# Gated linear attention: half of the diff projections between the scan's levels, one output norm for all chunks, half copies of k on ScalarE

## The chip, the cores and the metric

The kernel runs on one core of a Trainium2 chip. The metric is the device time of one execution in microseconds. Three runs of the kernel before took 2683.73, 2684.15 and 2686.27 us, so its time is the median, 2684.15 us.

## The reference

The reference computes two layers of a hybrid trunk on 640 tokens (128 context tokens and 512 latent tokens) of width 1024, in float32. A layer has a mixer and an MLP. The mixer projects the normed input once and splits the columns among three branches. Branch A is gated linear attention (GLA) over both directions, branch B is latent attention, branch C is differential attention. The three outputs are merged by sigmoid gates that are computed from the same input. What the change touches is the end of branch A and the start of branch C:

```python
def gla_branch(q, k, v, r, a_lr, w_a2, b_a, g_out, s0):
    ...
    o_f, s_f = gla_chunk_scan(q, k, v, g[:, :, 0], s0[:, 0])
    o_b, s_b = gla_chunk_scan(flip(q), flip(k), flip(v), flip(g[:, :, 1]), s0[:, 1])
    o = rms_norm(o_f + flip(o_b), g_out.astype(f32))
    y = o.reshape(B, S, W_A).astype(r.dtype) * jax.nn.silu(r)
...
(aq, ak, av, ar, aa, qd, kvd, kr, dq, dk, dv, gates) = jnp.split(h @ lp['w_in'], offsets, axis=-1)
q_c = rms_norm(dq.reshape(B, S, H_C, 2, D_C), lp['g_diff_q'])
k_c = rms_norm(dk.reshape(B, S, H_C, 2, D_C), lp['g_diff_k'])
...
g_a, g_b, g_c = jnp.split(jax.nn.sigmoid(gates), N_BRANCH, axis=-1)
merged = g_a * (y_a @ lp['w_o_gla']) + g_b * (y_b @ lp['w_o_mla']) + g_c * (y_c @ lp['w_o_diff'])
```

Inside a chunk the scan's decayed attention is exact: for each pair of positions the decay between them is a difference of running sums of g.

## The kernel before

Every float32 matmul against weights is done as three matmuls on a high and a low half of each operand (`mm3`, L101 to L103). The halves of a weight are made after its load: the high one by a cast on ACT (L94), the low one by a subtraction on DVE (L96). All DMAs of the parts shown here are issued by SP, in one queue.

The order of the work is the order in which the Python code emits it, refined by a scheduler that works by priorities when the program is built; at run time each engine takes its own list in order. Between the steps of a branch the code emits filling work for TensorE with `fill(n)`. It takes n pieces from a list of generators: first the four blocks of the gate r of branch A (`gla_r`), then blocks of the merge's gates (`gates_early`). A piece is 24 matmuls that fill one PSUM tile, of 384 columns for the first half of the tokens and 256 for the second, then a tanh on ACT and a store. What has not been emitted when the merge comes is computed there. A layer emits 49 pieces ahead of the merge, three after each chunk of the scan.

The scan of branch A goes through five chunks of 128 positions (`gla_chunk`), each of them through seven levels of halving block sizes. In a level POOL makes differences of the running sums (L509, L510), ACT takes their exponential (L511), DVE multiplies q (L518) and k (L524) by it, PE multiplies the two for four heads (L527) and DVE copies the result into the chunk's matrix under a mask (L531). At the last level, of block size one, half of k is only copied, on DVE (L522), and half of q is doubled on ACT (L520). At the chunk's end PE multiplies the matrix by v (L541) and q by the state (L543). Then the output norm follows: a square on ACT (L545), a sum on DVE (L547), an inverse root in twelve small operations on DVE (`rsqrt`, L123 to L130), the scaling (L551), four transposes on PE (L554), a load of the gate r into "ya" (L556), the product with it (L557), and the store (L558).

After the scan the diff attention starts with its first half of heads: the projections of k, of q and of v (`diff_proj`, fifteen steps of 24 matmuls of 256 columns, each with an eviction by ACT, L385), the norm and rotation of k and q (`diff_prep`), three filling pieces, and then scores and attention (L953).

Of the kernel before, what the change touches and what calls it, by code (L numbers as in the profile page):

```python
# [11 lines left out]
F32 = mybir.dt.float32  # L12
# [22 lines left out]
MLA_FILL = (1, 0, 1, 0, 0, 0, 1, 1, 1, 1, 1, 1, 1, 1, 1, 1)  # L35
DIFF_FILL = (0, 2)
# [16 lines left out]
    "gla_q": ("gla", 1), "gla_k": ("gla", 1), "gla_es": ("gla", 1), "gla_p": ("gla", 10), "gla_v": ("gla", 5),  # L53
    "wa2": ("gla", 1), "aT": ("gla", 2), "gla_t0": ("gla", 2), "gla_t1": ("gla", 2),
# [6 lines left out]
    "tabdq": ("dif", 1), "tabdk": ("dif", 1), "df_q": ("dif", 5), "df_k": ("dfr", 5), "df_v": ("dif", 10),  # L61
# [10 lines left out]
class Net:  # L72
# [316 lines left out]
    def gla_gates(self, l):  # L389
        nc = self.nc  # L390
        wa = self.S([33, 512], F32, "wa2")
# [3 lines left out]
        for tt in range(5):  # L395
            pt = self.P([128, 512], "gt")
            nc.tensor.transpose(pt[0:33, 0:128], self.aan[:, tt], self.ident)
            at = self.S([33, 128], F32, "aT")
# [26 lines left out]
    def gla_r(self, l, h, js):  # L425
        nc = self.nc
        for j in js:
            w = self.load_w(self.a["wfm"][l, 4 + j], [128, 8, 128])
            ws = [(w[0][:, k], w[1][:, k]) for k in range(8)]
            for c0, c1 in HALVES:  # L430
                p = self.P([128, 512], "f")
                n = c1 - c0
                self.gemm(p[:, :n], ws, h, c0, c1)
# [60 lines left out]
    def gla_chunk(self, l, c):  # L494
# [9 lines left out]
        for li, h in enumerate(LEVELS + (1,)):  # L504
# [45 lines left out]
        on = self.S([128, 4, 128], F32, "gla_o")  # L550
        nc.vector.tensor_tensor(on, o, r.unsqueeze(2).to_broadcast([128, 4, 128]), op=ALU.mult)  # L551
        p = self.P([128, 4, 128], "gt")
        for hd in range(4):
            nc.tensor.transpose(p[:, hd], on[:, hd], self.ident)  # L554
        y = self.S([128, 4, 128], F32, "ya")
        nc.sync.dma_start(y, self.yr[:, :, cs])  # L556
# [1049 lines left out]
```

## Time and profile before

| | |
|---|---|
| median of three runs | 2684.15 us |
| the profiled execution | 2684.53 us, its span 2682.7 us |
| PE busy | 2540.2 us (95%) |
| PEld busy (weight loads, beside PE) | 2429.5 us (91%) |
| DVE busy | 1712.2 us (64%) |
| ACT busy | 1142.2 us (43%) |
| POOL busy | 531.8 us (20%) |

The span is the time from the first to the last instruction on the chip; the 1.83 us beyond it lie around the program. An engine that is busy for 95% of the span can still be waiting for others for much of one stage, and another that is busy for 64% can be the one that is waited for there. So the shares are to be read by stage.

### The profile page before, as it was taken

The page shows a single profiled execution, that of the slowest core. Times are in us where ns is not written, and L with a number is a line of the kernel's source. Part 1 is how long each engine was busy: PE and PEld are TensorE (multiplying, and loading weights), DVE is VectorE, ACT ScalarE, POOL GpSimd, SP SyncE. Part 2 cuts the span into 40 slices and gives each one's busy share as a digit, 9 for nine tenths or more (in the row PEclk, how much of TensorE's full clock was granted, in tenths as well). Part 3 has the DMA queues.
Part 4 walks back from the last instruction along what each step waited for, and adds up shares of the span by engine and source line. Part 5 has one row for each costly group of instructions (what it writes and reads, how often), then busy time and mean ns, then how long its engine had stood idle before and what let it go on. Part 6 is the DMA issues. An engine that isn't in the chain of part 4 may idle for free.

```text
span 2682.7 us, 45820 instructions
## 1 busy us (share of the span) xinstructions
PE 2540.2 (95%) x17680; PEld 2429.5 (91%) x17680; DVE 1712.2 (64%) x3952; ACT 1142.2 (43%) x2287; POOL 531.8 (20%) x704
## 2 busy tenths in 40 slices
PE   6999997899998999999989999978999999999999
PEld 3988897789898999999989888878898999999999
DVE  6477649767688776766665775597685556333332
ACT  4476553356523342231335774533564334132231
POOL 3022115521032021020221211355100401010110
PEclk8999999999999999999999999999999999999999
DMA  6111212221275544444421112122113542222221
GB/s 247 44 51 63 66 62 73 72 76 56 84 257 199 162 138 153 149 150 150 150 77 54 44 57 80 49 80 78 60 57 129 192 143 78 79 72 79 71 79 48
DMA packets 112273, 268.87 MB, mean 100 GB/s; under 512 B 12534, under 2 KB 48374, under 8 KB 111288
## 3 DMA queue, kind: packets, MB, share of 16 engines
q1 hardware_dynamic: 112056, 265.95, 30.5%
q8 instruction: 139, 2.28, 0.4%
q14 instruction: 78, 0.64, 0.1%
HBM read 234.55 MB, written 31.36 MB: 99 GB/s over the span
## 4 chain that ended last, share of the span: by engine, by line
PE 70%; DVE 18%; ACT 5%; issue 3%; DMA 3%; POOL 1%; SPq 0%; DVEq 0%; ACTq 0%; POOLq 0%
PE g L103 17%; PE g L101 17%; PE g L102 17%; PE f L101 3%; PE f L103 2%; PE f L102 2%; DVE gla_z L518 2%; DVE wlo L96 2%; DVE mjunk L208 2%; PE y L991 1%; DVE gla_A L531 1%; PE g L787 1%; DMA modw<-wmod 1%; DVE gla_t L524 1%; PE g L983 1%
## 5 line engine op out<-in xcount | busy, mean ns | idle before, releaser
L96 DVE TENSOR_TENSOR wlo<-wraw,whi 128x1024 fp32r<-128x1024 f32 (+3 forms) x230 | 261.2, 1137 | 225.7 <-ACT whi L94 223.7
L94 ACT CAST whi<-wraw 128x1024 fp32r<-128x1024 f32 (+2 forms) x236 | 219.9, 932 | 398.5 <-PE g L102 306.5
L103 PE MATMUL g<-hh,wlo 128*128 128x384 f32 (+1 forms) x1056 | 331.2, 314 | 2.6 <-DVE wlo L96 2.6
L101 PE MATMUL g<-hh,whi 128*128 128x384 f32 (+1 forms) x1056 | 329.8, 312 | 1.9 <-ACT gth L1152 1.4
L102 PE MATMUL g<-hl,whi 128*128 128x384 f32 (+1 forms) x1056 | 329.7, 312 | 0.0
L1265 POOL TENSOR_TENSOR relu<-relu 128x256 f32<-128x256 f32 (+1 forms) x128 | 112.8, 882 | 801.4 <-ACT uh L1264 794.5
L208 DVE CUSTOM_DVE_ANT_0 mjunk<-modw,condb 128x1024 bf16<-128x1024 f32 x160 | 199.0, 1244 | 53.6 <-DMA modw<-wmod 52.9
L94 ACT CAST xhi<-xraw 128x1024 fp32r<-128x1024 f32 (+1 forms) x80 | 83.7, 1046 | 285.3 <-PE g L102 256.4
L103 PEld LDWEIGHTS g<-hh,wlo 128*128 128x128 f32 x1056 | 200.7, 190 | 3.3 <-DVE wlo L96 3.3
L101 PEld LDWEIGHTS g<-hh,whi 128*128 128x128 f32 x1056 | 201.0, 190 | 2.8 <-ACT gth L1152 1.8
L1214 DVE SCALAR_TENSOR_TENSOR x<-g,moda,x 128x256 f32<-128x256 f32 (+1 forms) x192 | 78.2, 435 | 193.3 <-PE g L103 193.3
L102 PEld LDWEIGHTS g<-hl,whi 128*128 128x128 f32 x1056 | 200.9, 190 | 0.1
L103 PE MATMUL g<-hh,xlo 128*128 128x384 f32 (+1 forms) x544 | 167.5, 308 | 0.0
L101 PE MATMUL g<-hh,xhi 128*128 128x384 f32 (+1 forms) x544 | 167.3, 307 | 0.0
L102 PE MATMUL g<-hl,xhi 128*128 128x384 f32 (+1 forms) x544 | 167.3, 307 | 0.0
L103 PE MATMUL g<-uh,wlo 128*128 128x384 f32 (+1 forms) x512 | 158.2, 309 | 0.0
L101 PE MATMUL g<-uh,whi 128*128 128x384 f32 (+1 forms) x512 | 158.2, 309 | 0.0
L102 PE MATMUL g<-ul,whi 128*128 128x384 f32 (+1 forms) x512 | 158.1, 309 | 0.0
L103 PE MATMUL g<-uh,xlo 128*128 128x384 f32 (+1 forms) x512 | 157.8, 308 | 0.0
L102 PE MATMUL g<-ul,xhi 128*128 128x384 f32 (+1 forms) x512 | 157.5, 308 | 0.0
L101 PE MATMUL g<-uh,xhi 128*128 128x384 f32 (+1 forms) x512 | 157.5, 308 | 0.0
L1201 POOL TENSOR_TENSOR x<-x,th 128x256 f32<-128x256 f32 x64 | 76.6, 1205 | 373.9 <-DVE th L1199 209.8
(449 smaller groups left out, 7859.3 us busy)
## 6 DMA issues: line engine op xcount, KB each, us to landing
modw<-wmod SPq DMA_DIRECT2D x80, 512.0 KB, 3.5
wraw<-w SPq DMA_DIRECT2D x64, 512.0 KB, 3.5
xraw<-w SPq DMA_DIRECT2D x64, 512.0 KB, 3.6
wraw<-wfm SPq DMA_DIRECT2D x62, 512.0 KB, 3.6
wraw<-wn SPq DMA_DIRECT2D x36, 512.0 KB, 3.6
wraw<-wo SPq DMA_DIRECT2D x48, 256.0 KB, 3.2
th<-gd SPq DMA_DIRECT2D x26, 320.0 KB, 3.1
gd<-gth SPq DMA_DIRECT2D x42, 192.0 KB, 1.9
```

What stands on the lines that cost most here:

```text
L94: nc.scalar.copy(hi, raw)
L96: eng.tensor_tensor(lo, raw, hi.bitcast(F32), op=ALU.subtract)
L101: mm(out, wh, xh, start=first, stop=False)
L102: mm(out, wh, xl, start=False, stop=False)
L103: mm(out, wl, xh, start=False, stop=last)
L208: nc.vector.tensor_tensor_reduce(out=junk, in0=w, in1=self.condb[:, s], scale=1.0, scalar=0.0, op0=ALU.mult, op1=ALU.add, accum_out=self.m ...
L518: nc.vector.tensor_tensor(q5[rs, :, :, u], qi[rs, :, :, u], d5[rs, :, :, u], op=ALU.mult)
L524: nc.vector.tensor_tensor(kt, k, dt, op=ALU.mult)
L531: nc.vector.copy_predicated(A, self.mask[:, li - 1].unsqueeze(1).to_broadcast([128, 4, 128]), p)
L1201: nc.gpsimd.tensor_tensor(mg[m][:, c0:c1], mg[m][:, c0:c1], t[:, c0:c1], op=ALU.add)
L1214: self.nc.vector.scalar_tensor_tensor(dst[:, p0:p1], p[:, p0 - c0:p1 - c0], self.moda[l][:, kind * 8 + m, s:s + 1], src[:, p0 - o:p1 - o], ...
L1265: nc.gpsimd.tensor_tensor(r[:, :n], r[:, :n], r[:, :n], op=ALU.mult)
```

## The change

The norm of the output leaves the chunk. A chunk now ends with a copy of its output into the place of its v, the square, and a sum that goes into one column of a common tile. After all chunks `gla_out` takes one inverse root for all and then scales, transposes, loads, multiplies and stores chunk by chunk. The three projections of the first half of the diff attention are emitted in steps after the levels 1, 3 and 5 of each chunk. Filling pieces can be left half done: a half is 12 matmuls, and every count of `fill` is now one of halves. Halves follow the levels 0, 2 and 4 and the chunk's end, so a chunk takes two whole pieces. The half copies of k are done by ACT. Some tiles change pools: the raw q and v of the first diff half to a pool that is open during the scan, and two tiles of the gates take the names of the scan's own.

```diff
 MLA_FILL = ...
-DIFF_FILL = (0, 2)
+DIFF_FILL = (0, 4)
+GLA_FILL = (0, 2, 4)
+GLA_PROJ = (1, 3, 5)
...
+    def gemm_part(self, out, ws, hs, c0, c1):
+        n = len(hs)
+        for k in range(n):
+            (wh, wl), (xh, xl) = ws[k], hs[k]
+            self.mm3(out, wh, wl, xh[:, c0:c1], xl[:, c0:c1], k == 0, k == n - 1)
+            if k == n // 2 - 1:
+                self.open_piece = True
+                yield
+                self.open_piece = False
+    def settle(self):
+        while self.open_piece:
+            self.fill(1)
...
-                    nc.vector.tensor_copy(k5[rs, :, :, 1 - u], ki[rs, :, :, 1 - u])
+                    nc.scalar.copy(k5[rs, :, :, 1 - u], ki[rs, :, :, 1 - u])
...
+            if li in GLA_PROJ:
+                while self.projq and next(self.projq[0], self) is self:
+                    self.projq.pop(0)
+            if li in GLA_FILL:
+                self.fill(1)
...
+        ov = self.v[c].rearrange("p (a b) -> p a b", a=4)
+        nc.scalar.copy(ov, o)
         sq = self.S([128, 4, 128], F32, "gla_o")
         nc.scalar.activation(sq, o, AF.Square)
-        ss = self.S([128, 4], F32, "gla_ss")
-        nc.vector.tensor_reduce(out=ss, in_=sq, axis=AX.X, op=ALU.add)
-        r = self.S([128, 4], F32, "gla_r")
-        self.rsqrt(r, ss, 1.0 / 128, 4)
-        ...
+        nc.vector.tensor_reduce(out=self.gss[:, c], in_=sq, axis=AX.X, op=ALU.add)
+
+    def gla_out(self):
+        r = self.S([128, 5, 4], F32, "gla_r")
+        self.rsqrt(..., self.gss..., 1.0 / 128, 20)
+        for c in range(5):
+            cs = slice(c * 128, c * 128 + 128)
+            ov = self.v[c].rearrange("p (a b) -> p a b", a=4)
+            on = self.S([128, 4, 128], F32, "gla_o")
+            nc.vector.tensor_tensor(on, ov, r[:, c].unsqueeze(2).to_broadcast([128, 4, 128]), op=ALU.mult)
+            p = self.P([128, 4, 128], "gt")
+            for hd in range(4):
+                nc.tensor.transpose(p[:, hd], on[:, hd], self.ident)
+            y = self.S([128, 4, 128], F32, "ya")
+            nc.sync.dma_start(y, self.yr[:, :, cs])
+            nc.vector.scalar_tensor_tensor(y, p, self.ghalf, y, op0=ALU.mult, op1=ALU.mult)
+            nc.sync.dma_start(self.yd[0][:, :, cs], y)
...
         for c in range(5):
             self.gla_chunk(l, c)
-            self.fill(3)
+            self.fill(1)
...
+        self.projq = [self.diff_proj(l, 0, i, h) for i in (1, 0, 2)]
         self.gla_chunks(l)
-        self.drain(self.diff_proj(l, 0, 1, h))
+        for g in self.projq:
+            self.drain(g)
+        self.gla_out()
+        self.settle()
...
-        self.drain(self.diff_proj(l, 0, 0, h))
         self.diff_prep(l, 0, 1)
         self.diff_prep(l, 0, 0)
-        self.drain(self.diff_proj(l, 0, 2, h))
-        self.fill(3)
+        self.fill(8)
         self.diff_attend(l, h)
```

How this stands in the lists of the engines is shown at three places. The line numbers of the changed kernel are higher (L96 is L99 there, L518 is L537, L524 is L543, L531 is L550, L547 is L572). The first place is DVE in the second half of the third chunk of the first layer. Before, the previous chunk's scaling and product with r (L551, L557) stand between the levels:

```order
L130 SCALAR_TENSOR_TENSOR gla_r<-rq_t_4976,gla_r 128x4
L518 TENSOR_TENSOR gla_z_4844<-gla_q,gla_t_5152 64x64x4
L551 TENSOR_TENSOR gla_o<-go,gla_r 128x512
L531 COPY_PREDICATED gla_A<-mask,go 128x512
L524 TENSOR_TENSOR gla_t_5156<-gla_k,gla_t_5152 128x512
L557 SCALAR_TENSOR_TENSOR ya<-gt,ghalf,ya 128x512
L518 TENSOR_TENSOR gla_z_4847<-gla_q,gla_t_5166 64x128x2 x2
L531 COPY_PREDICATED gla_A<-mask,go 128x512
L524 TENSOR_TENSOR gla_t_5170<-gla_k,gla_t_5166 128x512
L518 TENSOR_TENSOR gla_t_5185<-gla_q,gla_t_5180 64x256
L522 COPY gla_t_5184<-gla_k 64x256
L518 TENSOR_TENSOR gla_t_5185<-gla_q,gla_t_5180 64x256
```

After, only the sum of the previous chunk (L572) is left of it:

```order
L572 TENSOR_REDUCE gla_ss<-gla_o 128x4
L537 TENSOR_TENSOR gla_z_4856<-gla_q,gla_t_5519 64x32x8 x2
L543 TENSOR_TENSOR gla_t_5494<-gla_k,gla_t_5490 128x512
L99 TENSOR_TENSOR wlo<-wraw,whi 128x1024
L550 COPY_PREDICATED gla_A<-mask,go 128x512
L543 TENSOR_TENSOR gla_t_5523<-gla_k,gla_t_5519 128x512
L537 TENSOR_TENSOR gla_z_4859<-gla_q,gla_t_5559 64x64x4 x2
L537 TENSOR_TENSOR gla_z_4862<-gla_q,gla_t_5586 64x128x2 x2
L550 COPY_PREDICATED gla_A<-mask,go 128x512
L543 TENSOR_TENSOR gla_t_5563<-gla_k,gla_t_5559 128x512
L550 COPY_PREDICATED gla_A<-mask,go 128x512
```

The inverse root, the scaling, the product and the copies L522 are gone from the list here.

The second place is DVE behind the last chunk. Before, the end of the rsqrt of one chunk, its scaling and product, and then the sums for the norm of k (L896) and its low halves (L935):

```order
L129 SCALAR_TENSOR_TENSOR rq_t_5935<-rq_t_5935,rq_v_5933 128x4
L130 SCALAR_TENSOR_TENSOR gla_r<-rq_t_5935,gla_r 128x4
L551 TENSOR_TENSOR gla_o<-go,gla_r 128x512
L557 SCALAR_TENSOR_TENSOR ya<-gt,ghalf,ya 128x512
L1360 TENSOR_SCALAR ghalf<-vec 128x1
L896 TENSOR_REDUCE df_ss<-df_sq 128x4 x2
L935 TENSOR_TENSOR df_kl<-df_kc,df_k_6764 64x128
L935 TENSOR_TENSOR df_kl<-df_kc,df_k_6765 64x128
```

After, the end of the rsqrt for all chunks, then five scalings (L583) and five products with r (L589), and then the same sums (L929):

```order
L148 SCALAR_TENSOR_TENSOR rq_t_6211<-rq_t_6211,rq_v_6209 128x20
L149 SCALAR_TENSOR_TENSOR gla_r<-rq_t_6211,gla_r 128x20
L583 TENSOR_TENSOR gla_o<-gla_v,gla_r 128x512 x2
L589 SCALAR_TENSOR_TENSOR ya<-gt,ghalf,ya 128x512
L583 TENSOR_TENSOR gla_o<-gla_v,gla_r 128x512
L589 SCALAR_TENSOR_TENSOR ya<-gt,ghalf,ya 128x512
L583 TENSOR_TENSOR gla_o<-gla_v,gla_r 128x512 x2
L589 SCALAR_TENSOR_TENSOR ya<-gt,ghalf,ya 128x512 x3
L1395 TENSOR_SCALAR ghalf<-vec 128x1
L929 TENSOR_REDUCE df_ss<-df_sq 128x4 x3
```

All five chunks' products have moved ahead of the preparation of k and q.

The third place is SP's list at the end of the scan. Before, the stores of "ya" (L558) for the last three chunks and the load of "ya" (L556) for the last one, with stores of gates (L1153) and loads of weights (L91) between them; the other loads stand further up:

```order
L558 DMA yd_77<-ya 512x1x128
L556 DMA ya<-yr 128x4x128
L91 DMA wraw<-wn 128x1024
L1153 DMA gd_74<-gth 128x256
L1153 DMA gd_74<-gth 128x384
L91 DMA wraw<-wn 128x1024
L1153 DMA gd_74<-gth 128x256
L558 DMA yd_77<-ya 512x1x128
L1153 DMA gd_74<-gth 128x384
L91 DMA wraw<-wn 128x1024
L1153 DMA gd_74<-gth 128x256
L558 DMA yd_77<-ya 512x1x128
```

After, all five stores (L590) and the last three loads (L588) stand together, in turns; the loads of the first two chunks stand earlier:

```order
L94 DMA wraw<-wn 128x1024 x2
L1188 DMA gd_74<-gth 128x384
L94 DMA wraw<-wn 128x1024
L590 DMA yd_77<-ya 512x1x128 x2
L588 DMA ya<-yr 128x4x128 x2
L590 DMA yd_77<-ya 512x1x128 x2
L588 DMA ya<-yr 128x4x128
L590 DMA yd_77<-ya 512x1x128
```

The loads of chunks 2 to 4 have moved behind the stores of chunks 0 to 3. On PE the twenty transposes L586 stand in one group, ahead of the last four filling pieces.

## Rows read from the trace of the kernel before

**Rows 1.** The page, busy time of each engine

```profile
PE 2540.2 (95%) x17680; PEld 2429.5 (91%) x17680; DVE 1712.2 (64%) x3952; ACT 1142.2 (43%) x2287; POOL 531.8 (20%) x704
```

**Rows 2.** Busy time by stage, columns as its head names them

```profile
core 0: us, PE busy (x) PEld busy (x) DVE busy (x) ACT busy (x) POOL busy (x), PEclk, DMA share, GB/s
392.60:520.10 127.50, 101.14 (x713) 92.69 (x712) 117.37 (x223) 45.73 (x81) 69.55 (x98) 0.99 0.21 66
520.10:581.90 61.80, 60.08 (x469) 58.53 (x468) 35.37 (x98) 23.99 (x52) 15.29 (x28) 1.00 0.30 96
1722.80:1850.20 127.40, 102.73 (x713) 94.12 (x712) 117.18 (x223) 45.71 (x81) 69.49 (x98) 0.97 0.20 66
```

**Rows 3.** The waits in the scan: total, times, longest, us

```profile
ACT gla_t L511 <- POOL gla_t L510: 56.7, 24, 3.6
POOL gla_t L509 <- DVE gla_t L524: 23.3, 9, 3.6
```

**Rows 4.** Lines of DVE in the scan: busy us, mean ns, idle before

```profile
L522 DVE COPY gla_t<-gla_k 64x256 f32<-64x256 f32 x10 | 6.4, 637 | 0.0
L130 DVE SCALAR_TENSOR_TENSOR gla_r<-rq_t,gla_r 128x4 f32<-128x4 f32 x12 | 4.7, 394 | 0.0
...
L557 DVE SCALAR_TENSOR_TENSOR ya<-gt,ghalf,ya 128x512 f32<-128x512 f32 x4 | 3.0, 748 | 0.0
L547 DVE TENSOR_REDUCE gla_ss<-gla_o 128x4 f32<-128x512 f32 x4 | 2.7, 683 | 0.1
L551 DVE TENSOR_TENSOR gla_o<-go,gla_r 128x512 f32<-128x512 f32 x4 | 2.7, 683 | 0.1
...
L123 DVE TENSOR_SCALAR rq_v<-gla_ss 128x4 f32<-128x4 f32 x4 | 0.6, 160 | 0.0
```

**Rows 5.** Timeline of PE and PEld: start, length, instruction

```profile
394.46 0.28 PE L101 MATMUL g<-hh,whi 128*128 128x256 f32 x1
...
395.17 0.28 PE L101 MATMUL g<-hh,whi 128*128 128x256 f32 x1
...
401.20 0.34 PE L103 MATMUL g<-hh,wlo 128*128 128x384 f32 x1
...
402.59 0.34 PE L102 MATMUL g<-hl,whi 128*128 128x384 f32 x1
...
433.15 0.97 PEld L527 LDWEIGHTS go<-gla_z,gla_t 128*128 128x128 f32 x8
```

**Rows 6.** Lines of ACT in the scan

```profile
L520 ACT ACTIVATE gla_t<-gla_q 64x256 f32<-64x256 f32 x8 | 3.4, 424 | 0.0
L529 ACT COPY gla_A<-go 128x512 f32<-128x512 f32 x5 | 2.9, 578 | 0.0
```

**Rows 7.** Timeline of DVE, the last chunk's rsqrt

```profile
521.69 0.17 DVE L123 TENSOR_SCALAR rq_v<-gla_ss 128x4 f32<-128x4 f32 x1
...
523.87 0.16 DVE L130 SCALAR_TENSOR_TENSOR gla_r<-rq_t,gla_r 128x4 f32<-128x4 f32 x1
```

**Rows 8.** DMA issues: count, KB each, median us to landing

```profile
x<-gd SPq DMA_DIRECT2D x16, 320.0 KB, 5.7
...
ya<-yr SPq DMA_DIRECT2D x10, 256.0 KB, 3.3
yd<-ya SPq DMA_DIRECT2D x10, 256.0 KB, 2.6
```

**Rows 9.** Lines of DVE in the tail

```profile
L96 DVE TENSOR_TENSOR wlo<-wraw,whi 128x1024 fp32r<-128x1024 f32 x8 | 10.2, 1277 | 15.6 <-ACT whi L94 15.6
```

**Rows 10.** Busy time around a wait of PE, columns as in rows 2

```profile
472.20:474.50 2.30, 0.00 (x0) 0.00 (x1) 2.24 (x6) 1.46 (x4) 0.14 (x1) 0.94 0.46 178
474.50:477.50 3.00, 2.97 (x12) 2.97 (x13) 2.94 (x7) 0.63 (x1) 1.76 (x3) 0.50 0.01 4
```

**Rows 11.** Busy time in the merge of each layer

```profile
770.00:870.00 100.00, 87.78 (x578) 85.53 (x577) 82.34 (x132) 26.98 (x47) 41.51 (x32) 0.98 0.62 203
2070.00:2170.00 100.00, 99.78 (x688) 99.79 (x689) 57.81 (x97) 33.00 (x56) 32.65 (x31) 1.00 0.54 177
```

More of the change, by code (lines that the diff above doesn't have):

```diff
@@ L390, in gla_gates @@
         nc = self.nc
-        wa = self.S([33, 512], F32, "wa2")
+        wa = self.S([33, 512], F32, "gla_t2")
         nc.sync.dma_start(wa, self.a["wa2"][l])
@@ L432, in gla_r @@
                 n = c1 - c0
-                self.gemm(p[:, :n], ws, h, c0, c1)
+                yield from self.gemm_part(p[:, :n], ws, h, c0, c1)
                 t = self.S([128, 384], F32, "gth")
@@ L543, in gla_chunk @@
                 nc.tensor.matmul(o[:, hd], ei[:, hd], self.st[c][:, hd], start=False, stop=True)
+        ov = self.v[c].rearrange("p (a b) -> p a b", a=4)
+        nc.scalar.copy(ov, o)
         sq = self.S([128, 4, 128], F32, "gla_o")
         nc.scalar.activation(sq, o, AF.Square)
-        ss = self.S([128, 4], F32, "gla_ss")
-        nc.vector.tensor_reduce(out=ss, in_=sq, axis=AX.X, op=ALU.add)
-        r = self.S([128, 4], F32, "gla_r")
-        self.rsqrt(r, ss, 1.0 / 128, 4)
[L550 to L556, printed above, removed]
-        nc.vector.scalar_tensor_tensor(y, p, self.ghalf, y, op0=ALU.mult, op1=ALU.mult)
-        nc.sync.dma_start(self.yd[0][:, :, cs], y)
+        nc.vector.tensor_reduce(out=self.gss[:, c], in_=sq, axis=AX.X, op=ALU.add)
+    def gla_out(self):
+        nc = self.nc
+        r = self.S([128, 5, 4], F32, "gla_r")
+        self.rsqrt(r.rearrange("p a b -> p (a b)"), self.gss.rearrange("p a b -> p (a b)"), 1.0 / 128, 20)
+        for c in range(5):
[10 more added lines that the diff above has]
+            nc.sync.dma_start(self.yd[0][:, :, cs], y)
     def gla_chunks(self, l):
@@ L568, in gla_chunks @@
             self.qz[h] = z
+        self.gss = self.S([128, 5, 4], F32, "gla_ss")
         for c in range(5):
             self.gla_chunk(l, c)
-            self.fill(3)
+            self.fill(1)
     def mla_down(self, l, h):
@@ L880, in diff_proj @@
     def diff_proj(self, l, ch, i, h):
-        r = [self.S([128, 256], F32, f"df_{'qkv'[i]}") for t in range(5)]
+        r = [self.S([128, 256], F32, ("df_q", "df_k", f"df_v{ch}")[i]) for t in range(5)]
         self.raw[ch, i] = r
@@ L1084, in diff_attend @@
                 later.append(lambda ch=ch, yc=yc: store(ch, yc))
+        self.settle()
         self.ftag = "fg"
-        self.fill(1)
+        self.fill(2)
         for f in later:
@@ L1149, in gates_early @@
                 p = self.P([128, 512], self.ftag[c0 > 0])
-                self.gemm(p[:, :n], ws, h, c0, c1)
+                self.mid = True
+                yield from self.gemm_part(p[:, :n], ws, h, c0, c1)
                 t = self.S([128, 384], F32, "gth")
@@ L1366, in layer @@
         self.ftag = "ff"
-        self.mid, self.fillq, self.early, self.up, self.raw, self.rqd = False, [], set(), {}, {}, {}
+        self.mid, self.open_piece, self.fillq, self.early, self.up, self.raw, self.rqd = False, False, [], set(), {}, {}, {}
         fl, lat, latT, mla = ExitStack(), ExitStack(), ExitStack(), ExitStack()
@@ L1378, in layer @@
         self.pool_lo = False
-        self.fill(4)
+        self.fill(8)
         self.mla_latent(l)
@@ L1383, in layer @@
         mla.enter_context(self.pool("yb", "att", "mla"))
-        self.fill(1)
+        self.fill(2)
         self.drain(self.mla_keys(l, 0))
-        self.fill(1)
+        self.fill(2)
         self.mla_values(l, 0)
-        self.fill(1)
+        self.fill(2)
+        self.settle()
         ps.close()
@@ L1391, in layer @@
         self.mla_attend(l)
+        self.settle()
         for st in (mla, latT, ps):
@@ L1405, in layer @@
         self.gla_state(l)
-        self.fill(3)
+        self.fill(6)
+        self.projq = [self.diff_proj(l, 0, i, h) for i in (1, 0, 2)]
         self.gla_chunks(l)
-        self.drain(self.diff_proj(l, 0, 1, h))
+        for g in self.projq:
+            self.drain(g)
+        self.gla_out()
+        self.settle()
         for st in (gla, ps):
@@ L1414, in layer @@
         self.rope_tables((("dq", 0, 64, 0), ("dk", 64, 64, 0)))
-        self.drain(self.diff_proj(l, 0, 0, h))
+        nc.sync.dma_start(self.a["o_dv"][l, :, 0:256], self.raw[0, 2][4])
         self.diff_prep(l, 0, 1)
         self.diff_prep(l, 0, 0)
-        self.drain(self.diff_proj(l, 0, 2, h))
-        nc.sync.dma_start(self.a["o_dv"][l, :, 0:256], self.raw[0, 2][4])
-        self.fill(3)
+        self.fill(8)
         self.diff_attend(l, h)
-        while self.mid:
+        while self.mid or self.open_piece:
             self.fill(1)
```

10 lines of the change are left out of this document (5 added, 5 removed).

## The prediction

> **What bounds the kernel now.** I read the page first: TensorE (PE) is busy for 2540.2 of 2682.7 us [rows 1], so only stretches where it waits can give anything. The table by stage comes next [rows 2]. It has four stretches: in each layer from the end of the last state product (L480) to the last product of the scan (L541, "the scan"), and from there to the first score of the diff attention (L953, "the tail"). In the scan PE is busy for 101 of 127.5 us while VectorE (DVE) is busy for 117.4; in the tail PE is busy for 60.1 of 61.8. So the scan is bound by DVE and the tail by PE, and the second layer repeats it. The waits of the scan confirm the loop: ScalarE (ACT) waits 56.7 us for the differences that GpSimd (POOL) makes, and POOL 23.3 us for DVE's k product, whose buffer it refills [rows 3]. The lines of DVE show what loads it [rows 4].
>
> How much PE work is in there, without its waits? From start to start a matmul of 256 columns takes (395.17 - 394.46)/6 = 0.118 us, one of 384 columns (402.59 - 401.20)/8 = 0.174, a level's group of four 0.97 [rows 5]; for a product or a transpose of the same shape I take a quarter of that, 0.24, as an estimate. The order of before puts 172 filling matmuls of 384 columns, 170 of 256, 35 groups, 36 products and 16 transposes in the scan: 29.9 + 20.1 + 34.0 + 8.6 + 3.8 = 96 us, so 31 us of it are stalls. In the tail, where PE hardly waits, it fills the time.
>
> **The scan.** Three edits relieve DVE: the half copies of k go to ACT, the norm's rsqrt (six lines, twelve small operations a chunk) and L551/L557 leave the loop. By the rows that is 6.4 + 14.3 (the six lines from L130 to L123) + 2.7 + 3.0 = 26.4 us; two or three more low halves of weights (L96, 1.28 each in the tail [rows 9]) come in for the projections. DVE goes from 117.4 to about 95. PE gets 360 matmuls of the diff projections of 256 columns instead of about 100 filling ones: 121 x 0.174 + 120 x 0.118 + 360 x 0.118 + 34.0 + 8.6 = 120.3 us. Now PE is the longer of the two, and the scan is bound by PE. What stalls are left? The two opening levels of each chunk stand back to back, so their operands must be ready; new weight halves come in once or twice a chunk. I take 1 us a chunk: 125 us, 2.5 less than now. Below: no stall and the clock at full, 120. Above: half a microsecond at each of the 35 levels, beyond the 1 of the opening, 137. ACT takes 10 half copies at 0.42 (as its half multiplications of q, of the same shape), five o copies at 0.58, and 15 evictions of the projections, half as wide, at 0.58 at most [rows 6]: 16 us on an engine that was busy for 46 of 127 [rows 2], so hidden; uncovered they would sit in front of exponentials and count in the 137.
>
> **The tail.** What was hidden beside PE is now in the open. In the after order the 20 transposes of the output norm (L586) stand on PE ahead of the last four filling pieces, and the projections that once covered them are used up. From the last product (t = 0): o copy 0.58 and a square of the same shape on ACT, reduction 0.68 on DVE [rows 4], 2.1 with hand-offs. Then the rsqrt: twelve operations in steps of 0.2, from 521.69 to 524.03 before [rows 7], with one low half of 1.28 between: t = 5.7. Scaling, transposing and L589 for chunk 0 end at 8.0, for chunk 1 at 9.45. "ya" has two buffers, and yr is loaded into it. So chunk 2's load waits until chunk 0's store has landed, and chunk 4's until chunk 2's has: SP's order shows it. Store 2.6 and load 3.3 [rows 8]: the store leaves with L589 of chunk 0 and 0.05 of issue, lands at 10.65, the load at 13.95, L589 of chunk 2 ends at 14.75; the second round trip lands at 20.7, and L589 of chunk 4 ends at 21.6. The first filling matmul behind the transposes waits for it, and so does all of DVE's preparation of q and k, which is queued behind it. PE has 1.2 us of filling and 20 x 0.24 = 4.8 of transposes at most in that time, so it stands still for some 16 us.
>
> From t = 21.6 DVE has to do the preparation. The tail of before held 35.4 us of DVE work [rows 2], less 10.2 of low halves [rows 9] and 4.6 for its own last norm, 20.6; two low halves (2.6) and some 3 to 4 of hand-offs give 26 to 27. POOL's rotation of k has long run by then, since it starts from raw k. Filling (9 us left), tanh and transposes lie beside this. PE then starts at a lower clock: before, after 2.3 us without a matmul, the next 3.0 us had a granted clock of 0.50, the lower level of 1.2 GHz [rows 10]; I add 1 us. First score at 49.2 instead of 61.8: 12.6 less. Below, with every hop at the store's 2.6 and the preparation partly ahead, 45; above, 57, with hops of 5 us.
>
> The Trainium skill (TensorE: Matmul & The Clock Gate, section "HAM oscillation — how this bites in real kernels") says that gaps in which PE waits for transfers bring its clock down, and that each restart is paid again. That speaks against this change, which trades many short stalls for one long one; the row of 0.50 agrees in kind, and by it the price is 1 to 2 us a layer. The Trainium skill (DMA: Bandwidth & Descriptors, section "Anatomy of one DMA — SWDGE (gpsimd) path") gives 2.0 us fixed plus bytes over 436 GB/s for DMAs of another issuer, GpSimd, an estimate of 2.6 us for 256 KB: the store's row agrees, the load's is 0.7 above; by the page the two round trips would be 1.4 us shorter a layer.
>
> **What is moved later.** Half pieces are finer, but the counts don't match: 90 halves are 45 pieces where there were 49. Between the last state product and the first score that is 44 matmuls of 384 and 48 of 256 fewer, 13.3 us, which return in the merge as gate blocks; 15 projection matmuls of the second half come earlier, 1.8. Net 11.5 us more PE work behind the first score. Is there slack to take it? In 100 us of the merge PE is idle for 12 in the first layer, for none in the second [rows 11]. The blocks come in where PE waits only in part; I take 2 us absorbed in the first layer (0 to 6), none in the second, and 1 us a layer lost in the attention, which has fewer pieces to fill gaps with.
>
> **Sum.** A layer: -2.5 - 12.6 + 11.5 = -3.6, two layers -7.2, absorbed -2, attention +2: -7 on the profiled execution's 2684.53 (its span of 2682.7 and 1.8 around it), 0.4 above the median of 2684.15. That gives 2677, give or take 5 for small hand-offs.
>
> **Rivals.** (a) Dense: stalls of 2 us in the scan (122) and a tail of 46, 3 and 3.2 less than my terms in each layer, and 4 absorbed instead of 2: 2677 - 12.4 - 2 = 2663. For it: DVE, POOL and ACT all have a quarter of the scan free. Against it: 35 levels with a chain POOL, ACT, DVE, PE each. (b) No difference: the chain of a level, not DVE's sum, sets the pace in places; 3 us more stalls a layer give 2683. For it: ACT waits for POOL 24 times [rows 3], and POOL gets no less work. (c) Slower: the ya round trips. If a store or load takes 5 us, as x<-gd does with 320 KB under load (5.7) [rows 8], four hops cost 4 x 5 - 11.8 = 8.2 more a layer, all on the path: 2677 + 16 = 2693. It decides from hops of 3.8 us on, where 3.5 more a layer make the sum zero. Weight loads and gate stores are issued on the same queue around it, but SP itself waits in that order for ya, so little else is in flight; that speaks against it. (d) It doesn't unload DVE: small operations in the loop cost no time there because they sat in DVE's idle time, DVE stays the bound, and the scan grows by the added 25 us of PE work: 2677 + 2 x 27.5 = 2732. DVE's 92% against it.
>
> **Numbers.** Forecast 0.45, (a) 0.17, (b) 0.18, (c) 0.17, (d) 0.03. What a measurement here can tell from no change is 0.2%, 5.4 us, so faster means below 2678.8. Of the forecast 0.30 lies there, 0.14 within, 0.01 above; (a) is faster; (b) is 0.02 faster, 0.15 the same, 0.01 slower; (c) is 0.05 the same, 0.12 slower; (d) is slower. Faster 0.49, same 0.34, slower 0.17. The range for 8 in 10 goes from 2660, which holds most of (a), to 2693, the centre of (c); the forecast's own is 2672 to 2682.
>
> **What would show it.** In the scan, DVE busy for about 95 of 125 us and PE for some 120: right. A scan above 131 with ACT waiting for POOL: (b). In the tail, some 16 us of waiting on PE between the first and last L586, released by ya loads, and the first score about 49 us behind the last product: right; above 53, (c). The merge longer by 11 to 14 us in the second layer. The forecast is wrong if PE's stalls in the scan exceed 9 us, or if the tail isn't led by ya.

## The result: 2730 us, 1.7% slower, where 2677 was forecast

Four runs of the changed kernel took 2727.28 to 2732.42 us, median 2729.95; the runs of the kernel before beside them have a median of 2683.94. The ratio is 1.017 (95% interval 1.0152 to 1.0188). The profiled execution's span is 2726.5 us, 43.8 more than before. The prediction had 2677 and a range from 2660 to 2693.

The busy times by stage of the changed kernel, with columns as in [rows 2] (scan and tail of the first layer, then of the second, bounded by the same instructions):

```profile
core 0: us, PE busy (x) PEld busy (x) DVE busy (x) ACT busy (x) POOL busy (x), PEclk, DMA share, GB/s
392.50:536.10 143.60, 128.96 (x956) 125.26 (x955) 100.78 (x161) 59.60 (x112) 67.32 (x83) 0.94 0.15 52
536.10:582.30 46.20, 26.57 (x146) 23.74 (x145) 30.58 (x97) 12.90 (x28) 18.95 (x44) 0.74 0.38 118
1746.10:1888.40 142.30, 127.10 (x956) 123.25 (x955) 100.67 (x161) 59.47 (x112) 67.60 (x83) 0.96 0.15 52
1888.40:1934.60 46.20, 26.22 (x147) 23.38 (x146) 30.68 (x96) 13.02 (x29) 18.81 (x44) 0.74 0.38 119
```

The scan takes 143.6 and 142.3 us instead of 127.5, the tail 46.2 instead of 62. DVE has become free in the scan as meant (100.8 instead of 117.4 us [rows 2]), and yet the scan is longer. Cutting the rest at the last product of the attention with v and at the MLP's first squared ReLU shows where the 43.8 us went. I read the boundaries off the timelines, in us:

| stretch | before, layer 1 / 2 | after, layer 1 / 2 | difference |
|---|---|---|---|
| scan | 127.4 / 127.4 | 143.5 / 142.1 | +30.8 |
| tail, to the first score | 61.8 / 62.2 | 46.2 / 46.3 | -31.5 |
| diff attention | 136.5 / 136.2 | 139.6 / 139.3 | +6.2 |
| merge and output projection | 211.1 / 182.9 | 229.9 / 199.0 | +34.9 |
| MLP (and in layer 1 the next layer up to its scan) | 793.4 / 451.1 | 794.4 / 453.6 | +3.5 |

So scan and tail together are worth nothing, and the part behind the first score pays the whole difference.

Why is the scan long, when no engine is busy throughout? Its waits, columns as in [rows 3]:

```profile
ACT gla_t L530 <- POOL gla_t L529: 67.9, 31, 3.8
POOL gla_t L528 <- DVE gla_t L543: 55.2, 19, 5.4
DVE gla_z L537 <- ACT gla_t L530: 25.7, 19, 2.4
...
PE go L565 <- DVE gla_A L550: 11.3, 4, 3.6
```

In the kernel before, the profile puts POOL's waits for DVE down to small operations of the norm as well. Two of those lines, and DVE's wait for exponentials there:

```profile
POOL gla_t L509 <- DVE gla_r L130: 7.9, 5, 2.1
POOL gla_t L509 <- DVE rq_v L123: 6.6, 3, 2.2
DVE gla_z L518 <- ACT gla_t L511: 6.5, 4, 2.1
```

So the 23.3 us of [rows 3] are only a part of what POOL waited for DVE before. All lines of L509 that DVE ended give 48.0 us together, and those of L528 now 57.5. What has grown most is DVE's wait for exponentials, from 6.5 to 25.7 us. That is a ring: POOL makes the difference, ACT the exponential, DVE the products of q (L537) and k (L543), and only then is the exponent's tile free again. The timeline of a chunk's end shows how it reaches PE (start, length, engine, in brackets the wait):

```profile
476.38 0.67 DVE L543 TENSOR_TENSOR gla_t<-gla_k,gla_t 128x512 f32<-128x512 f32 x1
477.23 0.63 POOL L528 TENSOR_TENSOR gla_t<-gla_p 128x256 f32<-128x256 f32 x1 [3.27 <-DVE gla_t L543]
477.24 1.06 PE L546 MATMUL go<-gla_t,gla_t 128*128 128x128 f32 x8
477.82 0.63 POOL L529 TENSOR_TENSOR gla_t<-gla_p 128x256 f32<-128x256 f32 x1
478.48 0.63 ACT L530 ACTIVATE gla_t<-gla_t 128x512 f32<-128x512 f32 x1 [2.91 <-POOL gla_t L529]
479.14 0.87 DVE L537 TENSOR_TENSOR gla_z<-gla_q,gla_t 64x256 f32<-64x256 f32 x2 [2.09 <-ACT gla_t L530]
480.04 0.72 DVE L550 COPY_PREDICATED gla_A<-mask,go 128x512 f32<-128x512 uint8 x1
480.82 0.49 PE L565 MATMUL go<-gla_v,gla_A 128*128 128x128 f32 x2 [1.65 <-DVE gla_A L550]
```

PE ended the last level's matmuls at 478.3. The masked copy that takes them (L550) stands on DVE behind a q product of the next chunk, and this waits for its exponential until 479.14. PE has filling matmuls until 479.17, and its products then wait until 480.82. After the longer of these waits the granted clock falls: it was 0.66 over 420 to 430 and over 450 to 460 us, a mix of the levels of 2.4 and 1.2 GHz. The two waits, and the two stretches with columns as in [rows 2]:

```profile
421.90 0.80 PE L565 MATMUL go<-gla_v,gla_A 128*128 128x128 f32 x2 [3.62 <-DVE gla_A L550]
452.05 0.80 PE L565 MATMUL go<-gla_v,gla_A 128*128 128x128 f32 x2 [3.34 <-DVE gla_A L550]
...
420.00:430.00 10.00, 8.10 (x45) 8.09 (x46) 5.25 (x9) 4.60 (x9) 3.29 (x5) 0.66 0.04 14
450.00:460.00 10.00, 7.96 (x42) 7.96 (x43) 5.51 (x11) 4.84 (x9) 2.72 (x5) 0.66 0.05 20
```

The account of the first layer's scan closes with this within about a microsecond: 120.3 us of PE work as predicted, 143.6 - 129.0 = 14.6 idle, and at most (1 - 0.94) x 143.6 = 8.6 lost to the clock (the idle time is counted in it) make 143.5. The run without differences, below, has nearly the same PE work at full clock and shows it as 121.5 us.

### The profile page after: what moved, and what is told of

It is laid out like the page before. It is cut to its first block, busy times and chain, and to the rows that moved or that the text cites. A ratio compares the mean times of both kernels' runs of the same rounds, so it can differ in the third digit from the quotient of the medians.

```text
span 2726.5 us, 45718 instructions
## 1 busy us (share of the span) xinstructions
PE 2562.3 (94%) x17680; PEld 2456.2 (90%) x17680; DVE 1680.2 (62%) x3836; ACT 1154.5 (42%) x2317; POOL 534.8 (20%) x704
## 4 chain that ended last, share of the span: by engine, by line
PE 69%; DVE 14%; ACT 6%; DMA 5%; issue 3%; POOL 3%; SPq 0%; POOLq 0%; DVEq 0%; ACTq 0%
PE g L104 17%; PE g L105 16%; PE g L106 16%; PE f L104 2%; PE f L106 2%; PE f L105 2%; DMA modw<-wmod 1%; PE y L1024 1%; DVE gla_z L537 1%; DVE mjunk L227 1%; POOL gla_t L529 1%; PE g L820 1%; POOL gla_t L528 1%; DVE gla_A L550 1%; DVE sm_m L752 1%
## 5 line engine op out<-in xcount | busy, mean ns | idle before, releaser
L97 ACT CAST whi<-wraw 128x1024 fp32r<-128x1024 f32 (+2 forms) x236 | 219.8, 931 | 408.6 <-PE g L105 311.2
L99 DVE TENSOR_TENSOR wlo<-wraw,whi 128x1024 fp32r<-128x1024 f32 (+3 forms) x230 | 256.3, 1115 | 201.6 <-ACT whi L97 199.2
L104 PE MATMUL g<-hh,whi 128*128 128x256 f32 (+1 forms) x1040 | 327.0, 315 | 2.3 <-ACT whi L97 1.7
L106 PE MATMUL g<-hh,wlo 128*128 128x256 f32 (+1 forms) x1040 | 325.5, 313 | 3.5 <-DVE wlo L99 3.3
L105 PE MATMUL g<-hl,whi 128*128 128x256 f32 (+1 forms) x1040 | 322.6, 310 | 0.0
L97 ACT CAST xhi<-xraw 128x1024 fp32r<-128x1024 f32 (+1 forms) x80 | 83.4, 1042 | 282.0 <-PE g L105 258.6
```

The lines of the kernel that those rows point to most:

```text
L97: nc.scalar.copy(hi, raw)
L99: eng.tensor_tensor(lo, raw, hi.bitcast(F32), op=ALU.subtract)
L104: mm(out, wh, xh, start=first, stop=False)
L105: mm(out, wh, xl, start=False, stop=False)
L106: mm(out, wl, xh, start=False, stop=last)
```

## The experiments

**A tile more in the ring.** The first run moves the state's query out of the two tiles of the exponents; the other two give the k product or the exponents a third tile. The room for it comes from the tiles of the gate r, whose lines are left out here.

```diff
-            ei = self.S([128, 4, 128], F32, "gla_t0")          # e1
+            ei = self.S([128, 4, 128], F32, "gla_t2")
-    "gla_t0": ("gla", 2), "gla_t1": ("gla", 2),
+    "gla_t0": ("gla", 2), "gla_t1": ("gla", 3),                # e9
+    "gla_t0": ("gla", 3), "gla_t1": ("gla", 2),                # e10
...
```

> The changed kernel with one tile renamed: the decayed query for the state product (ei) leaves the ring of two exponent tiles (gla_t0) for that of gla_t2. Theory 1 (the scan is bound by the chain POOL difference, ACT exponential, DVE products, and at each chunk's end one of its two tiles is held until PE has done the state product): the scan falls from 143 us to about 130 in each layer, total about 2705. Theory 2 (the scan is bound by PE, its work and its clock, and DVE's waits only follow): the scan stays at 143 within 2 us, total 2730.

> The changed kernel with three tiles for the k product (gla_t1) instead of two; the room comes from one tile for the gate r instead of two, the other four chunks' r in tiles of the scan that are free by then (as in the run with five places). Theory 1 (PE now reaches a level's matmuls later, behind the projections, so the k product's tile comes free later, so DVE's list puts the next level's q product ahead of this level's k product, and both exponent tiles are held while DVE waits for the third exponential): in DVE's list q and k products alternate again, POOL's wait for the k product (55.2 us) falls to under 40, DVE's wait for exponentials (25.7) to under 12, the scan from 143 to 132 us or less, the total to 2700 to 2708 (the five places alone gave 2725.5). Theory 2 (the scan is held by PE's work and waits that only change their place): the scan stays within 3 us of 142, total 2720 or above.

> The same room spent on a third exponent tile (gla_t0) instead of a third tile for k. Theory 1: the k product still waits for its tile, DVE's list still puts q products of later levels ahead of it, the scan stays within 3 us of 142, total 2720 to 2730. Rival (too few exponent tiles are the cause themselves): the scan falls to 132 or less, total 2700 to 2708.

Measured: 2731.16 (scan 142.1 and 144.3 us), 2738.17 (150.0 and 149.9) and 2717.12 us (139.4 and 139.1). The profile of the third was taken in the slowest of its four executions, 2724.72 us. None of the three edits brought the scan to 132 us. The third k tile did not do what it was meant to do. On DVE, q products of a later level stand ahead of a level's own k product in 7 of 30 cases in the changed kernel, and still in 6 of 30 with the third k tile; in the kernel before it is none. POOL's wait for the k product (52.4 us, 55.2 without the edit) and DVE's for exponentials (30.1) did not fall as foreseen either. So the run leaves the first theory of its text untested. With the third exponent tile the order is disturbed in 24 of 30 cases, and the scan is the shortest of the three, so the count alone does not set the scan. The order on the engines is fixed when the program is built, and it is another one with each of these edits.

**A step of projections at the chunk's end.**

```diff
-GLA_PROJ = (1, 3, 5)
+GLA_PROJ = (1, 3, 6)
```

> The changed kernel with the last of the three projection steps of a chunk moved from behind level 5 to behind level 6, so that PE has 24 projection matmuls (2.8 us) between the last level's matmuls and the chunk's products, where it had about 6 filling ones. Theory 1 (PE's work is the same 120 us, and what lengthens the scan is PE's wait at each chunk's end for the last masked copy L550, which sits on DVE behind the next chunk's products of q, and the half clock that follows each of these waits): the wait of L565 for L550 (11.3 us on PE, before) falls to under 3, the clock of the scan rises to 0.98 or more, the scan takes 125 to 130 us instead of 143, total 2698 to 2706. Theory 2 (the chain of POOL, ACT and DVE is slower than PE, so a wait removed at one place comes back at the next level): the scan stays within 4 us of 143, with the waits at L546 instead, total above 2722.

Measured: 2725.12 us, scan 138.6 and 139.7. PE's wait for L550 is no more among its waits, yet it is idle for 138.6 - 123.8 = 14.8 us of the first layer's scan, as before the edit:

```profile
392.00:530.60 138.60, 123.79 (x949) 120.85 (x948) 101.66 (x160) 58.75 (x111) 65.51 (x91) 0.98 0.15 50
...
DVE gla_z L537 <- ACT gla_t L530: 23.3, 20, 2.4
...
PE g L104 <- ACT whi L97: 6.4, 3, 3.5
PE go L546 <- issue: 4.9, 2, 3.4
```

Both conditions of theory 1 came true (a wait for L550 under 3 us, a clock of 0.98), and the scan still did not fall to 130. The waits changed their place, as theory 2 has it, though only in part to L546: 6.4 us of them now are for weight halves from ACT (L97), which neither theory named. The gain of 2.5 to 5 us is what the clock (0.98 instead of 0.94 in the first layer) can give.

**No projections in the scan, and no differences in the scan.** The first run takes PE's additional work away (the projections come behind the scan); the second replaces POOL's two differences by a constant and so leaves the decays out.

```diff
-GLA_PROJ = (1, 3, 5)                                            # e4
+GLA_PROJ = ()
-            nc.gpsimd.tensor_tensor(d5[:, :, :, 1], ..., op=ALU.subtract)   # e13
-            nc.gpsimd.tensor_tensor(d5[:, :, :, 0], ..., op=ALU.subtract)
+            nc.gpsimd.memset(dt, -0.1)
```

> The changed kernel with the projections of the diff attention taken out from between the levels and done behind the last chunk; the norm for all chunks, the half pieces and the copies on ACT stay. PE has some 40 us less work in the scan. Theory 1 (chain of POOL, ACT and DVE): the scan still takes 110 to 125 us, with PE idle for a quarter of it or more. Theory 2 (PE is the bound): the scan falls by about the work taken out, to some 105 us or less, with PE busy throughout. The total is not decided by this alone, since 40 us of projections stand in the tail again: 2700 to 2735.

> The changed kernel with POOL's two differences of a level replaced by one filling with a constant, so the decays are left out; all other instructions stay. It shortens the chain POOL, ACT, DVE at each level by some 1 us and takes most of POOL's 60 us out of the scan. Theory 1 (the time from a freed exponent tile to the next exponential holds DVE's list, and through it the last masked copy that PE waits for): the waits of DVE for exponentials (25.7 us) and of PE at the chunk's end (11.3) fall to under half, the scan to 132 us or less, total 2705 or less. Theory 2 (DVE's list waits for PE's matmuls behind the projections, whatever POOL does): the scan stays above 138, total above 2718.

Measured: 2745.56 us with a scan of 114.6 and 114.0, and 2690.65 us with a scan of 123.9 in both layers. The rows of the scan, of the run without projections with PE's longest wait and then of the run without differences with its wait for exponentials:

```profile
392.30:506.90 114.60, 90.93 (x626) 83.47 (x625) 104.10 (x155) 49.42 (x91) 65.62 (x88) 0.96 0.14 46
...
PE go L546 <- DVE gla_t L543: 19.5, 19, 2.5
```

```profile
392.20:516.10 123.90, 121.53 (x954) 118.15 (x954) 92.43 (x163) 58.86 (x109) 26.88 (x49) 1.00 0.18 60
...
DVE gla_z L536 <- ACT gla_t L529: 13.1, 13, 1.4
```

Without the projections DVE is busy for 104 of 114.6 us, and PE waits most for its k product (19.5 us); PE is idle for a fifth of the scan, where theory 1 had a quarter. The total lies above the range given; the tail, where the projections now stand ahead of the output norm, takes 80.9 and 82.3 us. Without the differences PE is busy for 121.5 of 123.9 us at full clock: the scan that I had predicted (125). So neither PE's work nor DVE's alone holds the changed scan, but POOL's share of the ring together with PE's work.

A rival is that the order on DVE has changed, and not the time that a difference takes. For the run without differences the traces exclude it: later q products stand ahead of a k product at the same 7 of 30 places as in the changed kernel, in both layers, and the scan is 20 us shorter all the same. In the run without projections it is none of 30, as in the kernel before, so that run changes PE's work and the order together. One reservation stays: POOL's absence also makes DVE's own operations shorter (below; DVE is busy for 92.4 us instead of 100.8), so this run takes away two things at once.

**Half of POOL's differences on DVE.** The same, with the output kept.

```diff
-            nc.gpsimd.tensor_tensor(d5[:, :, :, 0], mid, f5[:, :, :, 0], op=ALU.subtract)
+            nc.vector.tensor_tensor(d5[:, :, :, 0], mid, f5[:, :, :, 0], op=ALU.subtract)
```

> The changed kernel with one of POOL's two differences of each level done by DVE instead (33 of 128x256, some 0.42 us each, 14 us on DVE). The output is the same. If the time from a freed tile to the exponential is what holds the scan, as the run without differences showed (124 us), and DVE's 100 us leave room for 14 more: scan 128 to 136, total 2700 to 2716. Rival (a difference on DVE waits in its list like the rest, and holds the chain as long): scan 141 or more, total 2726 or above.

Measured: 2712.21 us, scan 134.6 and 134.7. Scan and total lie where the text had them. With DVE busier than in the changed kernel (113.1 us) the scan is 9 and 7 us shorter, so shorter operations on DVE are not needed for the gain:

```profile
391.80:526.40 134.60, 122.95 (x955) 118.41 (x954) 113.13 (x199) 58.95 (x110) 38.96 (x49) 1.00 0.17 55
```

**The parts of the change alone.** The half copies on ACT in the kernel before; the norm put back into each chunk of the changed kernel.

> The kernel before with one edit of the change alone: the half copies of k on ACT. DVE is the bound of the scan there (117 of 127.5 us busy), and the edit takes 6.4 us from it and gives 4.2 to ACT. Theory A (DVE's busy time sets the scan): the scan falls by 4 to 6 us in each layer, total about 2675. Theory B (the chain through POOL and ACT sets it as much): under 2 us a layer, total above 2681.

> The changed kernel with the output norm back in each chunk, as before the change; projections between the levels, half pieces and copies on ACT stay. The scan then has some 20 us more DVE work (120 of the scan's time) beside PE's 120 plus the transposes, and the tail loses the 22 us up to the last product with r, of which 5 remain. Theory 1 (the single norm is what opens the gap in the tail, and DVE's load is not what bounds the changed scan): the scan grows by 0 to 6 us, the tail falls from 46 to about 32, total about 2705. Theory 2 (the single norm is what makes the new scan possible): the scan grows by 12 us or more, and the total is 2725 or above.

Measured: 2684.43 us (ratio 0.9995, 0.9986 to 1.0004) and 2722.90. The copies take 2 us from each scan (125.6 and 125.3), and the tail gives 1.5 of it back: theory B, nearly. So 6.4 us less work on the busiest engine gave 2. With the norm in the chunks the scan takes 156.5 us, 13 more, and the tail 34, 12 less, and the total is 7 us under the changed kernel's. Theory 2 had the scan right, theory 1 the tail, neither the total. So the single norm mostly carries its time from one stretch to the other, and what is left of the loss, some 39 of 46 us, lies by elimination with the projections and fillings between the levels and the four pieces that are missing.

**The missing pieces and the round trips.** Four filling pieces ahead of the chunks' norms (49 in all, as before the change); five places for the gate r.

```diff
+            if c < 4:                                            # e2, in gla_out
+                self.fill(2)
-            y = self.S([128, 4, 128], F32, "ya")                 # e3
+            y = self.S([128, 4, 128], F32, ("ya", "ya", "gla_t0", "gla_t0", "gla_t1")[c])
```

> The changed kernel with four more whole filling pieces, one ahead of each of the first four chunks' output norms, so that 49 pieces stand ahead of the merge again as before the change. Theory 1 (the four pieces that the change left for the merge cost their full PE time there, while PE stands still in the output norm): the part behind the first score shrinks by about 13 us in each layer, the tail grows by under 2, total about 2705. Theory 2 (the longer part behind the first score has other causes than the pieces): under 4 us less in each layer, total above 2722.

> The changed kernel with five places for the gate r in the output norm instead of two (the three others in tiles of the scan that are free by then), so no load waits for a store. Theory 1 (two round trips of store and load lead the tail, as the prediction had it): the last product with r ends about 13 us behind the last product of the scan instead of 22, the first score 37 to 39 us instead of 46, total about 2714. Theory 2 (the preparation of q and k on POOL, ACT and DVE is as long, and the round trips only fill its waits): the first score moves by under 3 us, total above 2724.

Measured: 2717.68 us; the merges fell by 14.7 and 13.5 us, so the pieces were most of what lengthened them (18.8 and 16.1), but the tail grew by 10. The transposes, now between the pieces, explain 2 us of that: the last product with r ended 24.2 us behind the last product of the scan instead of 22.4. Then a filling piece is late. Its tanh stands on ACT ahead of the first square for the norm of k, which starts 5.0 us behind that product; in the changed kernel one square is done by then and the next starts after 0.5 us. The rest of the 10 us is not traced further.

```profile
562.92 0.38 ACT L1189 ACTIVATE gth<-f 128x256 f32<-128x256 f32 x1 [9.55 <-issue]
563.20 0.41 ACT L930 ACTIVATE df_sq<-df_k 128x256 f32<-128x256 f32 x1
```

And 2725.54 us with five places: the last product with r came 16 us behind the last product of the scan instead of 22, but the first score only 2 us earlier. What is late next is a filling piece again. Its tanh stands on ACT ahead of the next square for the norm of k, and the piece only now runs:

```profile
536.80 0.41 ACT L928 ACTIVATE df_sq<-df_k 128x256 f32<-128x256 f32 x1
555.58 0.38 ACT L1187 ACTIVATE gth<-f 128x256 f32<-128x256 f32 x1 [18.37 <-PE f L106]
555.86 0.41 ACT L928 ACTIVATE df_sq<-df_k 128x256 f32<-128x256 f32 x1
```

**The addresses.** In the second layer's MLP all matmuls are the same, and it took 2.5 us longer.

```diff
...
+            nc.gpsimd.memset(self.S([128, 16], F32, "pad"), 0.0)   # 64 bytes more in the pool of small tiles
```

> The changed kernel with 64 bytes a partition added to its pool of small tiles, which is what the change took out of it (two tiles of the norm went to another pool), so that all pools behind it stand at their old addresses; one memset is added. In the MLP of the second layer, the same work in both kernels, the part up to the end took 453.6 us against 451.1 before, and matmuls of 384 columns came every 0.1751 us against 0.1735. Theory 1 (the moved addresses slow the 384-column matmuls): the spacing is 0.1735 again, that part takes 451, the merges are 2 to 4 us shorter, total 2718 to 2724. Theory 2 (addresses don't matter; something else differs): 453.6 and 0.1751 stay, total 2726 to 2732.

Measured: 2725.82 us. The spacing of 384-column matmuls went back to 0.1736 us (392 gaps in 120 us; 0.1735 before, 0.1751 after), but that of 256 columns rose from 0.1186 to 0.1194, the MLP took 452.6 and the merges 230.8 and 200.2. The run with the norm back in the chunks, whose two small tiles stand in their old pool again, agrees: 0.1735 us (395 gaps) and an MLP of 451.5. So moving the addresses moves the spacing by 0.9%, which is worth 1 to 2 us in this MLP. It does not explain the merges, which are no shorter with the old addresses (229.9 and 199.0 in the changed kernel).

**Versions that might win.** The single norm ahead of the projections behind the scan (e12); all helpful edits in the changed kernel (e16); the same with two more pieces ahead of the inverse root (e17), and with a half piece after each of the first four steps of the attention as well (e18). Two smaller sums (e2 with e3 and e5; e2 with e9) took 2702.81 and 2720.24 us.

> A version drawn from the runs so far: the changed kernel without projections and filling halves between the levels (three whole pieces after each chunk and the projections behind the scan, as in the kernel before), but with the single output norm, put ahead of the projections so that its chain runs beside them, with five places for the gate r, and the half copies on ACT; 49 pieces stand ahead of the merge. If the single norm is worth what DVE loses by it (the scan took 114 us in the run without projections, which had a piece less a chunk; 116 to 120 here), and the projections cover the norm's chain (tail 60 to 63, as before), it gains 6 to 11 us a layer: 2662 to 2674. Rival: the chain of the scan gets no faster with three pieces a chunk, or the norm's work delays the preparation of q and k behind the projections: 2680 or above.

> All edits that helped or may help together: the old addresses (64 bytes), one difference on DVE, the four filling pieces in the output norm, five places for the gate r, the projection step behind level 6. If the first two do what theory 1 and the split expect: scan 126 to 134, tail 50, merges as in the kernel before: 2665 to 2690. If neither does: 2700 or above, as with the three others (2702.8).

> The kernel with all helpful edits together, and two more whole filling pieces ahead of the output norm's inverse root, where PE stood still for 6 us in the changed kernel. If PE's waiting there is free to fill: tail 2 to 4 us longer, merge 7 shorter in each layer, total 2676 to 2682, under the kernel before. Rival (the transposes come later by the pieces, and the preparation of q and k with them): tail 6 or more longer, total 2684 to 2690.

Measured: 2697.82, 2685.97, 2685.80 and, for e18, 2685.74 us. Against the kernel before that is 1.0046 (1.0032 to 1.0059), 0.9999 (0.9990 to 1.0009), 1.0004 (0.9995 to 1.0013) and 1.0002 (0.9993 to 1.0011). None beats it. e12 has the shortest scan with its computation kept and all 49 pieces (117.4 and 116.0 us, and a tail of 62, as its text had them), and against the kernel before it loses about 9 us a layer in the attention and 5 in the merge; why is open. e16 came out within its range. In e17 the tail grew by 6 us a layer, in e18 the attention by 13 where 3 to 5 were expected, and both totals stayed as they were: the rivals.

## Why the prediction was wrong

- **The scan: the step that failed.** "I take 1 us a chunk: 125 us." This term, PE's stalls, was mis-sized, and with it the claim that the scan is bound by PE. PE's work was right within 1.2 us (120.3 expected, 121.5 at full clock in the run without differences). DVE's was 6 us above the forecast (95 expected, 100.8 measured), which is not what held the scan. But I bounded the stretch by the busy time of its longest engine and gave the ring 5 us in all; it cost 14.6 idle and up to 8.6 of clock in the first layer, 18 us more, and 15.2 and up to 5.7 in the second. PE's idle time did fall from 127.5 - 101.1 = 26.4 us [rows 2], but not to 5. Rival (b) named this mechanism and priced it at 3 us a layer, and its sign came: a scan above 131 us, with ACT waiting 67.9 us for POOL. My upper bound of 137 was still too low.
- **The tail: the time was right, its leader half right.** 49.2 predicted, 46.2 measured; the last product with r ended 22.4 us after the last product of the scan (21.6 predicted), and PE's waits up to the first filling matmul sum to 6.05 + 1.23 + 0.20 + 3.14 + 5.50 = 16.1 us (16):

```profile
543.30 1.97 PE L586 MATMUL gt<-ident,gla_o 128*128 128x128 f32 x8 [6.05 <-DVE gla_o L583]
546.50 1.08 PE L586 MATMUL gt<-ident,gla_o 128*128 128x128 f32 x4 [1.23 <-DVE gla_o L583]
547.78 1.09 PE L586 MATMUL gt<-ident,gla_o 128*128 128x128 f32 x4 [0.20 <-DVE gla_o L583]
552.01 1.09 PE L586 MATMUL gt<-ident,gla_o 128*128 128x128 f32 x4 [3.14 <-DVE ya L589]
558.60 0.55 PE L104 MATMUL f<-hh,whi 128*128 128x256 f32 x1 [5.50 <-DVE ya L589]
```

  The sum agrees, but the sign that I gave for it does not: between the first and the last L586 lie only 4.6 us of these waits, and 6.05 us come before them, from the inverse root. That the round trips of ya lead the tail was half right: with them gone, the last product with r came 6 us earlier and the first score only 2, because a filling piece on ACT's queue took their place. And POOL's rotation of k had not long run by then. One of its four tiles was done; the other three were finished only from 559.56 us on, behind the last product with r, because POOL waited for ACT's square, and this for DVE:

```profile
559.56 0.73 POOL L376 TENSOR_TENSOR df_k<-rt,rt 128x256 f32<-128x256 f32 x1 [10.96 <-ACT df_sq L928]
```

  So part of the agreement is luck. Rival (c) fell: the three loads that waited for stores landed after 3.1 to 3.2 us.
- **What is moved later: mis-sized.** Net 11.5 us a layer with 2 absorbed and 2 lost were expected, 23 in all; 44.6 came. The pieces cost their 14 us a layer (e2: 14.7 and 13.5), and nothing was absorbed in the first layer. The attention lost 3 us a layer although it has fewer matmuls, where I had it 1 us shorter. Merge and MLP grew by 38.4 us in both layers, of which e2 took back 28.2; the other 10 stay open. The addresses may be a part where the MLP is concerned, up to 2 us in the second layer, and not in the merges.
- **Rival (d)** gave 2732, near the time measured, by a mechanism that did not happen: DVE was busy for 101 of 143.6 us. That its number came close is chance.
- **The sum.** Scan +35.8, tail -6.3, the rest +21.6 against the terms: 51 us over the forecast, by the profiled execution's 2728.30 us.

What stays open is which link of the list on DVE makes the ring so slow. Shown is that it takes both the projections (114 us without) and POOL's differences (124 without, with the same order on DVE). Not separated is how much of the 114 is due to PE's work and how much to the order, which the projections change.

## What to carry to other kernels

A stretch whose engines hand tiles round in a ring need not be bounded by its busiest engine. Here 6.4 us of work taken off the busiest engine gave 2, and some 24 us of work put onto PE, which was idle for 26 us of the scan, used up only 12 of them. So before adding work, read in the new order of every engine's list who waits for whom, and let the waits have a term of their own. A single hand-over does not give that term: from the end of a k product to the end of the next exponential the timeline above shows 2.06 us (477.05 to 479.11), and 35 levels of it make 72 us, half of the scan. And filling work has a price where it is taken from: count the pieces before and after.

## What the runs showed of the hardware

DVE's q product of 64x256 has no fixed price. Those that write gla_z in the first layer's scan took 583 ns in the mean in the kernel before (POOL busy for 69.6 of 127.5 us [rows 2]), 510 in the changed one (67.3 of 143.6), 642 without projections (65.6 of 114.6), 494 with half of the differences on DVE (39.0 of 134.6) and 417 without differences (26.9 of 123.9): the denser POOL's work beside them, the longer.

```profile
L536 DVE TENSOR_TENSOR gla_z<-gla_q,gla_t 64x256 f32<-64x256 f32 x60 | 25.0, 417 | 13.5 <-ACT gla_t L529 13.1
...
L536 DVE TENSOR_TENSOR gla_t<-gla_q,gla_t 64x256 f32<-64x256 f32 x10 | 7.2, 721 | 0.1
```

The ten of the last level, of the same shape but written to gla_t, do not follow POOL's share of the stretch: they took 721 ns without differences and 422 in the kernel before. The Trainium skill (SBUF — State Buffer, section "SBUF: two separate sides") says that some operations of DVE and those of GpSimd lock a pair of ports against each other. The five means over gla_z agree in kind, those ten do not, and which operation waits for which no run here shows.

And moving the pools by 64 bytes a partition changes the spacing of 384-column matmuls by 0.9% (0.1751 to 0.1736 us), which I had not expected.
